# Weight tiles halved one tile after their fetch, and an output projection that starts with the attention heads, in a one-core decoder layer

## The chip, the cores and the metric

The kernel runs on one core of a Trainium2 chip. The metric is the device time of one launch in microseconds (us). Before the change it is 2632.16 us (median of three runs, 2631.33 to 2634.64).

The engines are named as the profile names them: PE multiplies matrices (PEld loads its stationary operand), DVE and POOL work elementwise, ACT scales, copies and takes sigmoids, and SP issues most of the DMAs. Each engine runs its own list of instructions strictly in the listed order; a semaphore makes an instruction wait for another engine or for a DMA.

## The reference

One trunk layer on `x` of 2048 tokens by 1024 channels, all in float32:

```python
a = rmsnorm(h, g_pre_mix)
u = a @ w_in                       # conv value | conv gate | q | k | v, 512 columns each
conv_out = silu(layernorm(causal_depthwise_conv31(val * sigmoid(gate)) + conv_b))
# stick-breaking attention, 8 heads of 64, no softmax; z = q k / 8:
log_1m = where(mask, log_sigmoid(-z), 0)
between = reverse_cumsum(log_1m) - log_1m
attn = where(mask, exp(log_sigmoid(z) + between), 0)
attn_out = headwise_rmsnorm(attn @ v, attn_norm_g)
y = concat([conv_out, attn_out]) @ w_out
h = h + rmsnorm(y, g_post_mix)
f_in = rmsnorm(h, g_pre_ffn)
f = (silu(f_in @ w_gate) * (f_in @ w_up)) @ w_down        # 2816 hidden channels
h = h + rmsnorm(f, g_post_ffn)
```

## The kernel before

**Precision.** [...] 

**Tiles and stages.** The tokens are worked in four groups `g` of 512. A table `PLAN` lists the main stages in order: `qkv` and `gv` are the input projection (`inproj`) of a group, `mix` gathers the two branches of a group, `out` is the output projection (`outproj`), and `fprep`, `c11` and `p4` are first parts of the feed-forward products. Each stage is a Python generator; a helper `beside` emits, between its steps, steps of three side generators: the attention (`attn`), the convolution (`taps`, then `convnorm`) and sums of feed-forward weights (`sums`). A step that needs a result first yields a `need`, and sides are emitted until it is there.

What is emitted earlier has priority, but the lists of the engines are made by a scheduler that simulates the engines and their buffers: the listed order can differ from the emitted one, and a small edit can move instructions hundreds of rows away. The hardware then follows the lists.

**Attention.** Work is counted in *scores*: one score is one tile of 128 queries against up to 512 keys of one head. It is two matmuls into `z` (L558, L559), two sigmoids on ACT (`om` L564, `A` L566), a scan on DVE (L568), a multiply on POOL (L569), four transposes of `A` on PE (`at`, L585), a split of those into `TH` and `TL` (L245, L246), and two matmuls into `o` (L590, L591). There are 320 scores, with four `om` buffers between them. "Dense" matmuls are those of the main stages: `inps`, `ops`, `c` (c11) and `p` (p4).

**Weights.** `Weights.next` hands out weight tiles of 128 by 1024. It calls `load_w` for up to `ahead` tiles beyond the one in use. `load_w` issues the DMA into `raw` (two buffers, L206), the copy to `wH` on ACT (L207) and, the first time a tile is used, the subtraction to `wL` on POOL (L211, one instruction of 1024 columns), whose result is also stored in DRAM (L213). At a later use of the same tile `wL` is loaded instead (L209). `half_w` does the same on 512 columns for `p4` (L222 to L224).

**The mixer.** `mix(g)` waits for `conv` and `attn` of its group, takes the two-buffered `xH`/`xL` tiles, and splits eight blocks: k = 0 to 3 from the convolution, loaded from DRAM into `m` (L519), and k = 4 to 7 from the attention, which lie on chip as `ma`. ACT makes `xH` (L523), DVE `xL` (L524). `outproj` multiplies by `w_out` in two column halves `e`; each half takes k = 0 to 3 first and k = 4 to 7 second. The first part is copied out on ACT (L688), the second is added on DVE (L690).

**The five products.** After the last output projection, `five` runs 44 blocks of Strassen-like products numbered 6, 5, 7, 4 and 3 (4 is left out where `p4` has it already). Its weights are the stored sums of pairs, (6, 5) and (7, 3); each pair is loaded into a `raw` tile (L1049), copied to `wH` (L1060) and subtracted on POOL (L1061), one block ahead. For the first blocks the remaining `residual` parts and `input_sums` are emitted between the products; `input_sums` ends in splits of `piece` (L802, L803). The tag `row` has four buffers: in `five` it holds one tile with `c11` and `p4` or a22 data per block (`ra`, loaded by L1043, L1116, L1117 and others), the `xr` and `junk` rows of a residual, and in the second half the `a22h` tile.

Of the kernel before, what the change touches and what calls it, by code (L numbers as in the profile page):

```python
# [18 lines left out]
P = 128  # L19
S = 2048  # L20
D = 1024
# [114 lines left out]
def layer_kernel(ctx: ExitStack, tc: tile.TileContext, x, xT, g_pre_mix, w_in, conv_w, conv_b, ln_g, ln_b,  # L136
# [61 lines left out]

    def load_w(w):

        src, n = w
        H = wp.tile([P, D], F32R, tag="wH", name="wH", bufs=3)
        L = wp.tile([P, D], F32R, tag="wL", name="wL", bufs=3)
        key = id(src), n
        raw = wp.tile([P, D], F32, tag="raw", name="raw")
        nc.sync.dma_start(raw, src[n])  # L206
        nc.scalar.activation(H, raw, AF.Copy)  # L207
        if key in kept:
            nc.sync.dma_start(L.bitcast(F32), kept[key])  # L209
            return H, L  # L210
        nc.gpsimd.tensor_tensor(L, raw, H.bitcast(F32), ALU.subtract)  # L211
        kept[key] = dp.tile([P, D], F32, name=f"wL_{len(kept)}")
        nc.sync.dma_start(kept[key], L.bitcast(F32))  # L213
        return H, L

    def half_w(w):

        src, n = w
        r = wp.tile([P, D], F32, tag="raw", name="raw")
        H = wp.tile([P, D], F32R, tag="wH", name="wH", bufs=3)  # L220
        L = wp.tile([P, D], F32R, tag="wL", name="wL", bufs=3)
        nc.sync.dma_start(r[:, 0:G], src[n][:, G:2 * G])  # L222
        nc.scalar.activation(H[:, 0:G], r[:, 0:G], AF.Copy)
        nc.gpsimd.tensor_tensor(L[:, 0:G], r[:, 0:G], H[:, 0:G].bitcast(F32), ALU.subtract)  # L224
        return H, L

    class Weights:


        def __init__(self, srcs, ahead=2, load=load_w):  # L230
            self.srcs = list(srcs)
            self.load = load
            self.tiles = []
            self.n = 0
            self.ahead = ahead

        def next(self):
            while len(self.tiles) < min(self.n + 1 + self.ahead, len(self.srcs)):
                self.tiles.append(self.load(self.srcs[len(self.tiles)]))
            self.n += 1  # L240
            return self.tiles[self.n - 1]

# [268 lines left out]
    def mix(g, tiles=None):  # L511

        yield need(("conv", g), ("attn", g))
        Hs, Ls = xtiles() if tiles is None else tiles()
        mc[g] = (Hs, Ls)
        for k in range(KT):
            if k < CB:
                m = ev("m")
                nc.sync.dma_start(m, conv[g][:, k, :])  # L519
            else:  # L520
                m = ma[g, k - CB]
            H = Hs[k // CB][:, k % CB, :]
            nc.scalar.activation(H, m, AF.Copy)  # L523
            nc.vector.tensor_tensor(Ls[k // CB][:, k % CB, :], m, H.bitcast(F32), ALU.subtract)  # L524
        done.add(("mix", g))
        yield 1
# [461 lines left out]
    with ExitStack() as E:  # L988
# [48 lines left out]
        def weights(g, i, j, A):  # L1037
# [9 lines left out]
            for ns in ((6, 5), (7, 3)):  # L1047
                r = wp.tile([P, D], F32, tag="raw", name="raw")
                nc.sync.dma_start(r, stored["S", i, j, ns].rearrange("p n t -> p (n t)"))  # L1049
                raws.append((r, ns))  # L1050
# [331 lines left out]
```

## Time and profile before

| what | value |
|---|---|
| median of the runs shown | 2632.16 us |
| time of the profiled execution | 2632.4 us |
| its span, first to last instruction | 2630.6 us |
| mean granted PE clock | 0.970 |
| PE busy | 2460.1 us, 94% |
| DVE busy | 1859.7 us, 71% |
| POOL busy | 1482.0 us, 56% |
| ACT busy | 1290.7 us, 49% |

The profile is one execution. Busy time counts an instruction from its start to its end; matmuls overlap, so PE can be busy without running at its peak. A row of a group reads: line, engine, operation, written tile, read tiles, shapes, count, busy time in total, mean of one in ns, and the idle time of the engine right before, with what ended it. In the chain of waits the work is followed back from the last instruction. "Granted clock" is the share of the full PE clock that the throttle passed.

By stretches, the stages lie so: mixed projections, attention and feed-forward parts from 0 to 1527 us, the last output projection to about 1586 us, `five` to about 2178 us, then the down projection.

### The profile page before, as it was taken

The page shows a single profiled execution, that of the slowest core. Times are in us where ns is not written, and L with a number is a line of the kernel's source. Part 1 is how long each engine was busy: PE and PEld are TensorE (multiplying, and loading weights), DVE is VectorE, ACT ScalarE, POOL GpSimd, SP SyncE. Part 2 cuts the span into 40 slices and gives each one's busy share as a digit, 9 for nine tenths or more (in the row PEclk, how much of TensorE's full clock was granted, in tenths as well). Part 3 has the DMA queues.
Part 4 walks back from the last instruction along what each step waited for, and adds up shares of the span by engine and source line. Part 5 has one row for each costly group of instructions (what it writes and reads, how often), then busy time and mean ns, then how long its engine had stood idle before and what let it go on. Part 6 is the DMA issues. An engine that isn't in the chain of part 4 may idle for free.

```text
span 2630.6 us, 35776 instructions
## 1 busy us (share of the span) xinstructions
PE 2460.1 (94%) x11156; PEld 1970.1 (75%) x11156; DVE 1859.7 (71%) x2409; ACT 1290.7 (49%) x2395; POOL 1482.0 (56%) x1844
## 2 busy tenths in 40 slices
PE   8889989997999999999999989889999999999998
PEld 6777867785777778777788767667777777887886
DVE  5787569977999676687765538877776665557556
ACT  4455546656564565557666643333322224444543
POOL 6654587557765656548534406675534434557556
PEclk9999989998999999989999989999999999999999
DMA  9999869986798788856777646887665557668654
GB/s 343 330 305 308 286 221 314 358 285 219 255 350 262 251 306 277 293 168 224 264 255 231 203 152 216 315 270 242 206 210 184 193 199 271 194 196 271 210 190 170
DMA packets 289182, 657.32 MB, mean 250 GB/s; under 512 B 33888, under 2 KB 42080, under 8 KB 288992
## 3 DMA queue, kind: packets, MB, share of 16 engines
q1 hardware_dynamic: 264704, 622.01, 70.8%
q10 hardware_dynamic: 24288, 33.04, 3.5%
q8 instruction: 88, 1.44, 0.2%
q14 instruction: 102, 0.84, 0.1%
HBM read 460.92 MB, written 193.99 MB: 249 GB/s over the span
## 4 chain that ended last, share of the span: by engine, by line
PE 61%; DVE 15%; DMA 10%; POOL 6%; issue 5%; ACT 2%; SPq 1%; POOLq 0%; DVEq 0%; ACTq 0%
PE b L755 16%; PE dps L755 13%; PE c L755 9%; DVE om L568 3%; PE at L585 3%; DVE cv L473 2%; PE inps L253 2%; PE inps L255 2%; PE inps L257 2%; PE p L755 2%; PE o L591 2%; PE z L558 2%; PE ops L686 1%; PE ops L684 1%; PE ops L685 1%
## 5 line engine op out<-in xcount | busy, mean ns | idle before, releaser
L569 POOL TENSOR_TENSOR A<-A,om 128x512 f32<-128x512 f32 (+2 forms) x320 | 314.4, 983 | 356.5 <-DVE om L568 314.8
L568 DVE TENSOR_TENSOR_SCAN om<-om,one,z 128x513 f32<-128x513 f32 (+2 forms) x320 | 351.5, 1112 | 115.1 <-ACT A L566 103.1
L1061 POOL TENSOR_TENSOR wL<-raw,wH 128x512 fp32r<-128x512 f32 x176 | 257.2, 1489 | 283.7 <-ACT wH L1060 283.7
L473 DVE SCALAR_TENSOR_TENSOR cv<-glu,cw,cv 128x512 f32<-128x512 f32 x464 | 346.4, 746 | 5.8
L1241 DVE TENSOR_TENSOR xL__22087<-t__22089,xH__22086 128x512 fp32r<-128x512 f32 x154 | 197.8, 1293 | 159.2 <-ACT xH__22086 L1240 159.2
L1239 POOL TENSOR_TENSOR xL__22085<-t__22088,xH__22084 128x512 fp32r<-128x512 f32 x154 | 207.6, 1353 | 176.1 <-ACT xH__22084 L1238 175.5
L253 PE MATMUL inps<-xH,wL 128*128 128x512 f32 x640 | 262.2, 410 | 4.3 <-DVE qkL L246 4.0
L255 PE MATMUL inps<-xH,wH 128*128 128x512 f32 x640 | 259.0, 405 | 0.0
L257 PE MATMUL inps<-xL,wH 128*128 128x512 f32 x640 | 258.6, 405 | 0.0
L564 ACT ACTIVATE om<-z 128x512 f32<-128x512 f32 (+2 forms) x320 | 171.0, 536 | 164.9 <-DVE z L561 67.3
L246 DVE TENSOR_TENSOR TL<-at,TH 128x512 fp32r<-128x512 f32 (+1 forms) x320 | 189.2, 598 | 85.4 <-ACT TH L245 84.7
L755 PE MATMUL dps<-xH__22084,xL__22087 128*128 128x512 f32 x616 | 241.6, 392 | 6.8 <-DVE xL__22087 L1241 5.6
L755 PE MATMUL dps<-xL__22085,xH__22086 128*128 128x512 f32 x616 | 241.3, 392 | 3.9 <-POOL xL__22085 L1239 3.9
L755 PE MATMUL dps<-xH__22084,xH__22086 128*128 128x512 f32 x616 | 241.0, 391 | 0.0
L839 POOL TENSOR_TENSOR sum<-sum 128x512 f32<-128x512 f32 x132 | 172.2, 1305 | 104.3 <-DMA sum<-in_w_down_dram 37.5
L207 ACT ACTIVATE wH<-raw 128x1024 fp32r<-128x1024 f32 x156 | 165.6, 1062 | 104.1 <-DMA raw<-in_w_in_dram 42.7
L245 ACT ACTIVATE TH<-at 128x512 fp32r<-128x512 f32 (+1 forms) x320 | 167.7, 543 | 90.8 <-PE at L585 82.5
L1238 ACT ACTIVATE xH__22084<-t__22088 128x512 fp32r<-128x512 f32 x154 | 97.1, 631 | 232.8 <-POOL xL__22085 L1239 145.0
L585 PE MATMUL at<-idr,A 128*128 128x128 f32 x1088 | 194.2, 283 | 10.9 <-ACT ma L625 3.6
L585 PEld LDWEIGHTS at<-idr,A 128*128 128x128 f32 x1088 | 143.7, 146 | 48.8 <-POOL A L569 5.9
L566 ACT ACTIVATE A<-z 128x512 f32<-128x512 f32 (+2 forms) x320 | 167.5, 537 | 21.3 <-PE at L585 19.6
L558 PE MATMUL z<-K,QL 128*128 128x512 f32 (+2 forms) x320 | 132.4, 415 | 29.4 <-DVE om L568 24.0
(303 smaller groups left out, 6283.3 us busy)
## 6 DMA issues: line engine op xcount, KB each, us to landing
wL<-wL SPq DMA_DIRECT2D x156, 512.0 KB, 4.7
raw<-in_w_in_dram SPq DMA_DIRECT2D x80, 512.0 KB, 5.9
t__22089<-u SPq DMA_DIRECT2D x154, 256.0 KB, 2.8
c<-c ACTq DMA_DIRECT2D x88, 256.0 KB, 3.9
t__22088<-wd SPq DMA_DIRECT2D x88, 256.0 KB, 2.9
K<-kd SPq DMA_DIRECT2D x80, 256.0 KB, 4.5
V<-vd SPq DMA_DIRECT2D x80, 256.0 KB, 4.1
u<-accf SPq DMA_DIRECT2D x22, 768.0 KB, 4.1
```

Of the source, the lines that this page charges most:

```text
L246: nc.vector.tensor_tensor(L, ps, H.bitcast(F32), ALU.subtract)
L253: nc.tensor.matmul(ps, WL[:, kc], aH[t](k), start=k == 0, stop=False)
L255: nc.tensor.matmul(ps, WH[:, kc], aH[t](k), start=False, stop=False)
L257: nc.tensor.matmul(ps, WH[:, kc], aL[t](k), start=False, stop=k == KT - 1)
L473: nc.vector.scalar_tensor_tensor(to, gl[c][:, k:k + G], cw[:, c, k:k + 1], a, ALU.mult, ALU.add))
L568: nc.vector.tensor_tensor_scan(r, r, z[:, 0:1].to_broadcast([P, w + 1]), one, ALU.mult, ALU.bypass)
L569: nc.gpsimd.tensor_tensor(a[:, 0:w], a[:, 0:w], om[:, G - w + 1:G + 1], ALU.mult)
L585: nc.tensor.transpose(pt[:, j * P:(j + 1) * P], u["A"][j][:, b * P:(b + 1) * P], id32)
L755: return nc.tensor.matmul(ps, a, b, skip_group_check=True, **flags)
L1061: nc.gpsimd.tensor_tensor(l, t, f32(h), sub)
L1239: nc.gpsimd.tensor_tensor(WL, w, f32(WH), sub)
L1241: nc.vector.tensor_tensor(UL, t, f32(UH), sub)
```

## The change

1. `load_w` only allocates and fetches. The halving is put into a closure `halves`, which `Weights.next` calls one tile later: up to `ahead - 1` tiles beyond the one in use instead of `ahead`. For `c11` (`ahead` = 1) it is called for the tile in use.
2. The subtraction on POOL is done in pieces of 512 columns instead of one of 1024.
3. `half_w` becomes `load_w` with an offset.
4. `mix` issues the four loads of `m` first, then splits the attention blocks k = 4 to 7, then the convolution blocks k = 0 to 3.
5. `outproj` takes k = 4 to 7 first in both column halves, and fetches its weight tiles in that order.
6. In `five` the (7, 3) pair is loaded into a `row` tile, and only the (6, 5) pair into `raw`.

```diff
-    def load_w(w):
+    def load_w(w, lo=0):
         src, n = w
+        raw = wp.tile([P, D], F32, tag="raw", name="raw")
         H = wp.tile([P, D], F32R, tag="wH", name="wH", bufs=3)
         L = wp.tile([P, D], F32R, tag="wL", name="wL", bufs=3)
-        key = id(src), n
-        raw = wp.tile([P, D], F32, tag="raw", name="raw")
-        nc.sync.dma_start(raw, src[n])
-        nc.scalar.activation(H, raw, AF.Copy)
-        if key in kept:
+        m = D - lo
+        nc.sync.dma_start(raw[:, 0:m], src[n][:, lo:D])
+        key = id(src), n, lo
+        known = key in kept
+        if known:
             nc.sync.dma_start(L.bitcast(F32), kept[key])
-            return H, L
-        nc.gpsimd.tensor_tensor(L, raw, H.bitcast(F32), ALU.subtract)
-        kept[key] = dp.tile([P, D], F32, name=f"wL_{len(kept)}")
-        nc.sync.dma_start(kept[key], L.bitcast(F32))
-        return H, L
+        def halves():
+            nc.scalar.activation(H[:, 0:m], raw[:, 0:m], AF.Copy)
+            if known:
+                return
+            for i in range(0, m, G):
+                ks = slice(i, i + G)
+                nc.gpsimd.tensor_tensor(L[:, ks], raw[:, ks], H[:, ks].bitcast(F32), ALU.subtract)
+            if not lo:
+                kept[key] = dp.tile([P, D], F32, name=f"wL_{len(kept)}")
+                nc.sync.dma_start(kept[key], L.bitcast(F32))
+        return H, L, halves
...
         def next(self):
             while len(self.tiles) < min(self.n + 1 + self.ahead, len(self.srcs)):
                 self.tiles.append(self.load(self.srcs[len(self.tiles)]))
             self.n += 1
-            return self.tiles[self.n - 1]
+            while self.made < min(self.n + self.ahead - 1, len(self.srcs)):
+                self.tiles[self.made][2]()
+                self.made += 1
+            return self.tiles[self.n - 1][:2]
...
-        for k in range(KT):
-            if k < CB:
-                m = ev("m")
-                nc.sync.dma_start(m, conv[g][:, k, :])
-            else:
-                m = ma[g, k - CB]
+        ms = [ev("m") for _ in range(CB)] + [ma[g, p] for p in range(CB)]
+        for k in range(CB):
+            nc.sync.dma_start(ms[k], conv[g][:, k, :])
+        for k in (*range(CB, KT), *range(CB)):
...
-        wts = Weights([(w_out, n) for n in range(KT)])
+        order = range(CB - n, -1, -n)
+        wts = Weights([(w_out, CB * e + kp + i) for e in range(2) for kp in order for i in range(n)])
         for e in range(2):
             es = slice(e * G, (e + 1) * G)
-            for kp in range(0, CB, n):
+            for kp in order:
...
-                    if kp == 0:
+                    if kp == order[0]:
...
             for ns in ((6, 5), (7, 3)):
-                r = wp.tile([P, D], F32, tag="raw", name="raw")
+                r = wp.tile([P, D], F32, tag="raw", name="raw") if ns[0] == 6 else row("raw2")
```

The lists of the engines move in many places. Three of them matter below.

ACT at the second mixer (`mix(1)`), the copies from `m` and `ma` to `xH`. Before, they stand together, with a few instructions of the attention among them:

```order
L564 ACTIVATE om<-z 128x384
L523 ACTIVATE xH<-m 128x512
L523 ACTIVATE xH<-ma 128x512 x4
L564 ACTIVATE om<-z 128x512
L523 ACTIVATE xH<-m 128x512
L245 ACTIVATE TH<-at 128x512
```

Now three of the `ma` copies stand some 90 rows ahead of that, and the fourth 16 rows behind these three:

```order
L568 ACTIVATE om<-z 128x384
L251 ACTIVATE TH<-at 128x512 x2
L568 ACTIVATE om<-z 128x512
L527 ACTIVATE xH<-ma 128x512 x3
L214 ACTIVATE wH<-raw 128x1024
```

The `m` copies are at the old place:

```order
L568 ACTIVATE om<-z 128x512
L251 ACTIVATE TH<-at 128x512 x2
L527 ACTIVATE xH<-m 128x512 x3
L251 ACTIVATE TH<-at 128x512
L527 ACTIVATE xH<-m 128x512
L570 ACTIVATE A<-z 128x384
```

So four of the eight copies left the place at which the output projection begins, and the other four stayed.

PE at the end of the last `c11`, the last dense matmuls ahead of the end of the attention. Before, 4 scores of 320 are listed behind the last of these rows:

```order
L755 MATMUL c_17039<-xL,wH 128x512
L590 MATMUL o<-TH,V 128x512
L591 MATMUL o<-TL,V 128x512
L585 MATMUL at<-idr,A 128x128 x4
L590 MATMUL o<-TH,V 128x512
```

Now 12 scores are listed behind it, and the last transposes of the convolution too (`cps`):

```order
L760 MATMUL c_17089<-xL,wH 128x512
L509 MATMUL cps<-idr,cs 128x128 x4
L594 MATMUL o<-TH,V 128x512
L595 MATMUL o<-TL,V 128x512
L589 MATMUL at<-idr,A 128x128 x2
```

So the dense work runs ahead of the attention by eight scores more at this point. Counted through the two lists of PE, the stretches of more than six scores with neither a dense matmul nor `tps` transposes in them, together with the one at the end, are, before, 19 scores (105 to 124), 8 (220 to 228) and 4 (316 to 320); now 16 (108 to 124), 14 (217 to 231) and 12 (308 to 320).

ACT in `five`, around the last split of a `piece`. Before:

```order
L802 ACTIVATE e__18249<-piece 128x512
L1060 ACTIVATE wH<-raw 128x512 x4
L802 ACTIVATE e__18249<-piece 128x512
L1060 ACTIVATE wH<-raw 128x512 x2
L802 ACTIVATE t__19439<-sumin 128x512
```

Now:

```order
L807 ACTIVATE e__18299<-piece 128x512
L1065 ACTIVATE wH<-raw_18600 128x512 x2
L1065 ACTIVATE wH<-raw 128x512 x2
L807 ACTIVATE e__18299<-piece 128x512
L807 ACTIVATE t__19489<-sumin 128x512
```

Counted from the start of `five`, 22 pairs of `wH` copies stood ahead of the last split of a `piece`, and 23 do now; each of the four splits has one pair more ahead of it.

More of the change, by code (lines that the diff above doesn't have):

```diff
@@ L197, in layer_kernel @@
     kept = {}
[L199 removed]
+    def load_w(w, lo=0):
         src, n = w
+        raw = wp.tile([P, D], F32, tag="raw", name="raw")
         H = wp.tile([P, D], F32R, tag="wH", name="wH", bufs=3)
         L = wp.tile([P, D], F32R, tag="wL", name="wL", bufs=3)
[L204 to L225 removed]
+        m = D - lo
[3 more added lines that the diff above has]
+        if known:
+            nc.sync.dma_start(L.bitcast(F32), kept[key])
+        def halves():
[9 more added lines that the diff above has]
+        return H, L, halves
+    def half_w(w):
+        return load_w(w, G)
     class Weights:
@@ L234, in __init__ @@
             self.n = 0
+            self.made = 0
             self.ahead = ahead
@@ L1047, in weights @@
             for ns in ((6, 5), (7, 3)):
-                r = wp.tile([P, D], F32, tag="raw", name="raw")
+                r = wp.tile([P, D], F32, tag="raw", name="raw") if ns[0] == 6 else row("raw2")
                 nc.sync.dma_start(r, stored["S", i, j, ns].rearrange("p n t -> p (n t)"))
```

4 lines of the change are left out of this document (2 added, 2 removed).

## The prediction

> **What bounds the kernel now.** I read the page first, then the table by stretches, then the waits and the order in time of the stretches in which PE is not full.
>
> ```profile
> span 2630.6 us, 35776 instructions
> PE 2460.1 (94%) x11156; PEld 1970.1 (75%) x11156; DVE 1859.7 (71%) x2409; ACT 1290.7 (49%) x2395; POOL 1482.0 (56%) x1844
> ```
>
> PE is busy for 94% of the span, and the change neither adds nor removes a matmul. So it can only act on PE's idle time, 2630.6 - 2460.1 = 170 us, and on the clock that PE is granted. The execution took 2632.4 us, 1.8 more than its span and 0.2 more than the median of the runs, 2632.16; I count from 2632.4.
>
> The table by stretches tells where PE falls behind (columns: stretch, length, then busy time and count of PE, PEld, DVE, ACT and POOL, granted clock, DMA share, GB/s):
>
> ```profile
> 342.30:370.30 28.00, 20.75 (x79) 16.75 (x77) 23.11 (x29) 13.97 (x29) 19.08 (x23) 0.76 0.72 230
> 605.50:645.90 40.40, 31.62 (x143) 21.97 (x142) 33.00 (x50) 25.95 (x56) 32.69 (x59) 0.87 0.66 203
> 645.90:666.40 20.50, 14.49 (x58) 10.20 (x57) 18.51 (x27) 12.67 (x26) 11.84 (x20) 0.92 0.61 199
> 1124.10:1143.70 19.60, 16.12 (x59) 10.88 (x58) 17.68 (x28) 11.73 (x23) 9.80 (x16) 0.74 0.71 216
> 1320.00:1386.00 66.00, 66.00 (x324) 54.12 (x323) 45.91 (x62) 40.01 (x73) 20.25 (x49) 1.00 0.75 249
> 1492.70:1503.50 10.80, 8.44 (x36) 6.04 (x35) 6.98 (x7) 7.68 (x15) 4.08 (x9) 0.84 0.70 233
> 1700.00:1730.00 30.00, 21.91 (x88) 16.95 (x86) 26.18 (x33) 10.08 (x19) 17.57 (x13) 0.90 0.91 311
> ```
>
> Where attention and dense work are mixed, as from 1320 to 1386, PE is full at clock 1.00. It falls behind in three kinds of places: at the three mixers inside the attention (from 342, 646 and 1124), in stretches of attention alone (605 to 646, 1493 to 1504), and in the first blocks of `five` (1700 to 1730).
>
> A stretch of attention alone shows in the groups of PE within it: no dense line is among its larger groups, and 16 scores pass (L559 x16).
>
> ```profile
> L585 PE MATMUL at<-idr,A 128*128 128x128 f32 x58 | 11.1, 296 | 1.3 <-POOL A L569 1.3
> L558 PE MATMUL z<-K,QL 128*128 128x512 f32 (+3 forms) x17 | 8.8, 518 | 5.3 <-DVE om L568 5.3
> L559 PE MATMUL z<-K,QH 128*128 128x512 f32 (+3 forms) x16 | 6.7, 421 | 0.0
> ```
>
> PE waits most for the scan (L568) that gives an `om` buffer back: here the chain through ACT, DVE and POOL sets the pace.
>
> **The change, part by part.** *The mixers.* These rows show the first one (ACT and PE, in order of time) and the second:
>
> ```profile
> 344.72 0.63 ACT L523 ACTIVATE xH<-m 128x512 fp32r<-128x512 f32 x1 [5.70 <-DMA m<-conv]
> 345.25 0.96 ACT L245 ACTIVATE TH<-at 128x512 fp32r<-128x512 f32 x2
> 345.89 0.79 PE L590 MATMUL o<-TH,V 128*128 128x512 f32 x1 [2.74 <-ACT TH L245]
> 350.27 2.18 ACT L523 ACTIVATE xH<-ma 128x512 fp32r<-128x512 f32 x4
> 649.16 0.63 ACT L523 ACTIVATE xH<-m 128x512 fp32r<-128x512 f32 x1 [2.60 <-DMA m<-conv]
> 650.57 0.50 PE L684 MATMUL ops<-wH,xL 128*128 128x512 f32 x1 [2.27 <-DVE xL L524]
> ```
>
> ACT runs in order, so its 5.70 us wait for the convolution's load also held the attention's `TH`, and PE with it. The loss of a mixer is its idle time plus the share of its busy time that the clock took: (28.00 - 20.75) + 20.75 x 0.24 = 12.2 us at the first, (20.50 - 14.49) + 14.49 x 0.08 = 7.2 at the second, (19.60 - 16.12) + 16.12 x 0.26 = 7.7 at the third, 27 together. At the first mixer four head copies (2.18 us) and a `TH` (0.96) now stand ahead of the first copy from `m`: 3.1 of the 5.70 us, 55%, so 6.7 of 12.2. At the second the four head copies have left the place, while the load and its wait stay: I take half, 3.6. At the third the four loads are listed one by one among other DMAs, as before: a third, 2.6. Sum 13 us saved. Bounds: 0, if the load gates the in-order queue all the same, and 27.
>
> [...]
>
> *The fourth mixer*, after the attention, splits three head blocks, four `m` and the last head block, eight copies as before:
>
> ```profile
> 1525.89 2.18 ACT L523 ACTIVATE e__17216<-m 128x512 fp32r<-128x512 f32 x4
> ```
>
> The first product can start behind the first copy in both kernels; the last head block is copied eighth, 8 x 0.545 = 4.4 us on, when PE has nine slow matmuls behind it. Zero, at most 1 us lost.
>
> *The order of dense work and attention.* The scheduler's list has moved. By the counts beside the lists above, the stretches of scores without dense work grow from 19 + 8 + 4 = 31 to 16 + 14 + 12 = 42. In the mixed part a score costs PE its own work. Row prices: a 512-wide matmul 285.29 / 1212 = 0.235 us, a transpose 0.60 / 4 = 0.15 us:
>
> ```profile
> 1879.29 285.29 PE b L755 x1212
> 606.62 0.60 PE L585 MATMUL at<-idr,A 128*128 128x128 f32 x4
> ```
>
> A score is four matmuls and four transposes, 0.94 + 0.60 = 1.54 us. Alone it takes 40.40 / 16 = 2.53 us. So each bare score wastes 0.99 us, and 11 more of them cost 11 us, most at the end of the attention (8 more) and behind the first half of the third output projection (6 more). Bounds: 0, if the other engines catch up elsewhere; 16, by the dearer pace of 10.80 / 4 = 2.70 us and three scores more in the stretches with `tps`. That half an output projection can run before the convolution is done gives nothing further: it is already in these counts.
>
> *The halves one tile later.* In the lists the copies hardly move: a `wH` copy stands on average 4.8 scores ahead of its first matmul before, 5.0 now, and as far behind its load as before. PE's cover is three tiles of weights. Zero. If they were late, ACT's wait for `raw` would be late next:
>
> ```profile
> ACT wH L207 <- DMA raw<-in_w_in_dram: 42.7, 14, 6.0
> L211 POOL TENSOR_TENSOR wL<-raw,wH 128x1024 fp32r<-128x1024 f32 x50 | 120.3, 2407 | 54.6 <-ACT wH L207 53.5 <-DMA kd<-qkH 1.0
> L224 POOL TENSOR_TENSOR wL<-raw,wH 128x512 fp32r<-128x512 f32 x22 | 28.4, 1296 | 5.6 <-ACT wH L223 5.3 <-ACT om L564 0.2
> ```
>
> *The narrower pieces* make one POOL instruction of 2407 ns into two of 1296: 185 ns more, 50 times, 9 us of POOL. POOL is idle 44% of the span; what hides it is that idle time, and without cover it would be 9. In the bare stretch POOL is busy 32.69 of 40.40, so I take 1.
>
> *The (7, 3) pair in `row`.* In `five` PE and SP wait for the halving of weights:
>
> ```profile
> PE b L755 <- POOL wL L1061: 14.0, 7, 6.0
> SPq L1049 <- POOL wL L1061: 72.2, 31, 8.9
> 1726.73 0.63 ACT L802 ACTIVATE e__18249<-piece 128x512 fp32r<-128x512 f32 x1 [12.13 <-DVE piece L918]
> 1727.27 1.13 ACT L1060 ACTIVATE wH<-raw 128x512 fp32r<-128x512 f32 x2
> 1730.89 0.79 PE L755 MATMUL b<-xH__17525,wL 128*128 128x512 f32 x1 [6.00 <-POOL wL L1061]
> ```
>
> The longest PE wait, 6.00 us, is a pair whose copies stood on ACT behind a split that waited 12.13 us for DVE. With one pair more ahead of each such split that wait should go. But DVE is busy 26.18 of 30.00 us there and is late next: I take 5 of the 14.0 us. Bounds: 14 saved; and 9 lost, since `row` now holds one tile more per block and SP already waits for its buffers:
>
> ```profile
> SPq L1043 <- DVE sumf L1068: 9.4, 4, 3.6
> ```
>
> **Sum:** -13 - 5 + 11 + 1 = -6, so 2632.4 - 6 = 2626 us. All terms at their good ends give -41, all at their bad ends +35.
>
> **The rivals.** *Slower: the end of the attention decides.* Twelve bare scores at the end instead of four, and six more behind the third mixer, while the loads of `m` gate ACT as before: 11 + 1 us lost, nothing saved, 2644. For it: the `m` loads stand at the same place of SP's list at mixers two and three, and a lost score cannot be hidden once the dense work is gone. Against it: the 5.70 us wait of the first mixer has work ahead of it now. It decides as soon as mixers and `five` together give less than 12 us.
>
> *It cancels: 2632.* The mixers give 7 and `five` 4, and the bare scores take that back. For it: gains and losses come from the same shift, dense work ahead of attention; also the halving does not do what its words say, since the lists place it where it was.
>
> *Much faster: 2602.* The mixers give 22 of their 27 us because the clock stays up, `five` gives 9, and the bare scores cost nothing because DVE, with fewer splits at the mixers, passes the scores faster: 2632.4 - 31. Against it: DVE is busy 33.00 of 40.40 us in the bare stretch, where no mixer takes its time.
>
> **How the numbers follow.** Forecast 2626 (own range 2619 to 2629): 0.36. Much faster: 0.10. Cancelling: 0.28. Slower: 0.26. About 0.2%, 5 us, is what a measurement of this kernel can tell from no change, so faster is 0.36 + 0.10 = 0.46, same 0.28, slower 0.26. The range reaches from the edge of the much faster case to just past the slower one: 2606 to 2645.
>
> **What would show each step.** At the first mixer the wait of ACT's copy from `m` should be under 3 us and PE's wait for `TH` gone; at the second the wait of 2.27 us for `xL` may stay, with the clock up behind it. Before the last output projection PE should show 12 scores without a `c` matmul, some 30 us instead of 11. In `five`, PE's wait for `wL` should be under 9 us and the one of 6.00 us absent; waits for DVE should have grown. POOL's pieces should take near 1296 ns. The prediction is wrong if the scores of the bare stretches take less than 2.2 us, if SP blocks on `row` buffers so that PE waits for the (7, 3) pair, or if the granted clock of the span falls below 0.970.

## The result and the profile after

The changed kernel takes 2647.64 us (median of four runs, 2645.83 to 2655.61), the kernel before, run beside it, 2631.74 (2630.92 to 2634.64). The ratio is 1.0063 with a 95% interval of 1.005 to 1.0075: by the ratio 16.6 us slower, where I had forecast 6 us faster. The time also lies outside my range, 2606 to 2645.

The head of the page of the changed kernel:

```profile
span 2645.3 us, 35841 instructions
PE 2462.8 (93%) x11156; PEld 1969.2 (74%) x11156; DVE 1840.2 (70%) x2409; ACT 1293.5 (49%) x2395; POOL 1487.6 (56%) x1894
```

The work is the same; PE's idle time has grown from 170 to 182 us, and the granted clock is 0.972. The table by stretches of the changed kernel (columns: stretch, length, busy time and count of PE, PEld, DVE, ACT and POOL, granted clock, DMA share, GB/s):

```profile
315.00:345.00 30.00, 29.29 (x144) 23.57 (x143) 21.80 (x28) 21.66 (x41) 26.35 (x35) 1.00 0.81 279
576.00:597.00 21.00, 7.52 (x24) 5.88 (x24) 7.66 (x9) 4.64 (x9) 16.04 (x23) 0.64 0.59 197
610.00:652.40 42.40, 32.83 (x143) 22.93 (x142) 32.18 (x49) 26.62 (x57) 34.01 (x59) 0.85 0.72 224
652.40:678.40 26.00, 20.70 (x90) 15.91 (x89) 21.36 (x31) 12.92 (x24) 13.61 (x22) 0.91 0.65 203
1144.00:1155.90 11.90, 8.96 (x28) 6.12 (x27) 11.24 (x16) 9.11 (x18) 7.40 (x13) 0.71 0.78 271
1490.00:1514.30 24.30, 19.75 (x92) 12.82 (x91) 18.75 (x22) 18.25 (x36) 14.32 (x33) 1.00 0.55 185
1700.00:1730.00 30.00, 26.04 (x111) 20.88 (x110) 26.18 (x30) 10.00 (x18) 21.99 (x15) 0.89 1.00 359
```

The first mixer (from 315) hardly holds PE: 29.29 of 30 us busy at clock 1.00. (The output projection behind it waits once more, for a weight; see below.) But a hole of 21 us stands at 576, where PE is busy 7.52 us. The waits at the second and third mixers (652, 1144) are much as they were.

Two traces whose lists differ cannot be laid beside each other by the clock on the wall. I compared them at equal work of PE: each row of PE is given the price that it has where PE is full (the lower quartile of the time to the next row, by form, in the trace of before), and the prices are summed. Every kernel here comes to 2261 to 2263 us of work that way. Elapsed time minus work is *lost time*, and it can be told by stretches that hold the same amount of work in each kernel. The borders in the next table are 475, 540, 935, 1240 and 1290 us of work; in the kernel before they lie at 581, 688, 1154, 1484 and 1564 us. Each row of the table is worked out from one profiled execution. Two executions of one and the same edit (b_heads and its repeat) differ by at most 2.4 us in a column. That is a single pair, and the profiled execution need not be a typical one: in b_heads (2623.04 us, median 2629.38), heads_slot (2619.49, 2628.07) and b_wide (2650.32, 2662.03) it was the fastest of its runs. So the columns tell where time goes, and the ratios of the runs tell how much.

| kernel | to 475 | 475 to 540, second mixer | 540 to 935, third mixer | 935 to 1240 | 1240 to 1290, end of attention | rest | all |
|---|---|---|---|---|---|---|---|
| before, lost time | 98.8 | 41.5 | 71.8 | 24.3 | 30.5 | 84.6 | 351.4 |
| the change, against before | -23.2 | +14.3 | +10.8 | +2.3 | +8.1 | +1.5 | +13.8 |

So the change has a large gain first, 23.2 us up to the second mixer, and then gives back 14.3 there, 10.8 on the way to the third mixer and 8.1 at the end of the attention. The stretch of the second mixer, in the kernel before and in the changed one (their waits and clock differ, the work of PE is the same):

```profile
581.30:687.80 106.50, 85.94 (x396) 64.17 (x395) 85.94 (x122) 61.95 (x121) 79.09 (x123) 0.92 0.73 234
558.00:678.80 120.80, 90.37 (x393) 67.51 (x392) 85.97 (x122) 64.54 (x124) 82.36 (x127) 0.86 0.68 216
```

The hole at 576 us, seen on PE in order of time, the rows with a wait ahead of them (the last part of a row is the idle time and what ended it):

```profile
583.98 0.80 PE L689 MATMUL ops<-wH,xL 128*128 128x512 f32 x1 [8.04 <-DVE glu L430]
593.69 1.09 PE L627 MATMUL po<-idr,ot 128*128 128x128 f32 x4 [5.49 <-DVE ot L619]
```

And on POOL at the same time:

```profile
572.37 1.27 POOL L844 TENSOR_TENSOR sum<-sum 128x512 f32<-128x512 f32 x1
579.56 1.26 POOL L844 TENSOR_TENSOR sum<-sum 128x512 f32<-128x512 f32 x1 [5.92 <-DMA sum<-in_w_gate_dram]
580.78 0.86 POOL L573 TENSOR_TENSOR A<-A,om 128x384 f32<-128x384 f32 x1
...
582.99 0.21 POOL L429 COPY glu<-glu 128x30 f32<-128x30 f32 x1
```

This is a chain of queues. POOL has a sum of feed-forward weights (L844, work of the side generator `sums`, needed only in the last products, which start at 1594 us) at the head of its list, and waits 5.92 us for the load. Behind it stand the attention's products (L573) and a small copy of the convolution (L429). DVE's `glu` (L430) waits 8.09 us for that copy, and the output projection needs a PSUM bank of the kind that `glu` reads from (in the code both take theirs from the tag `mm`). So PE waits 8.04 us, and the dense work that could fill the time has run out. The row of 5.49 us is the same once more: the head norm's `ot` waits for `ss` from POOL (DVE's own wait is 0.85 us, the row on POOL runs from 590.13 us for 1.64), which stands behind further sums of 1.29 and 1.26 us.

An earlier wait comes from the same queue. In the first output projection PE waits 5.73 us for the low half of a `w_out` tile (the high half `wH` is ACT's copy of the tile, the low half `wL` is the tile minus `wH`, and a product is three matmuls, here `wH` by `xL`, `wH` by `xH` and `wL` by `xH`); no such row is in the kernel before. The rows on PE and POOL:

```profile
366.59 0.79 PE L691 MATMUL ops<-wL,xH 128*128 128x512 f32 x1 [5.73 <-POOL wL L219]
```

```profile
352.36 10.01 POOL L368 TENSOR_TENSOR xcol<-xcol,rb 128x512 f32<-128x512 f32 x8
...
365.27 4.96 POOL L219 TENSOR_TENSOR wL<-raw,wH 128x512 fp32r<-128x512 f32 x4
```

In POOL's order the halving of this tile, the sixth of `w_out`, stands behind 10 us of scaling for a later input projection (`xcol`). In the kernel before it stands behind the same block (subtraction at 394.16 us, `xcol` from 380.69 to 391.72), but there PE comes to the tile later and does not wait. So a part of PE's early lead is lost again at once.

### The profile page after: what moved, and what is told of

It reads as the page before. It is cut to its first block, busy times and chain, and to the rows that moved or that the text cites. A ratio compares the mean times of both kernels' runs of the same rounds, so it can differ in the third digit from the quotient of the medians.

```text
span 2645.3 us, 35841 instructions
## 1 busy us (share of the span) xinstructions
PE 2462.8 (93%) x11156; PEld 1969.2 (74%) x11156; DVE 1840.2 (70%) x2409; ACT 1293.5 (49%) x2395; POOL 1487.6 (56%) x1894
## 5 line engine op out<-in xcount | busy, mean ns | idle before, releaser
L573 POOL TENSOR_TENSOR A<-A,om 128x512 f32<-128x512 f32 (+2 forms) x320 | 312.5, 977 | 340.8 <-DVE om L572 310.3
L1066 POOL TENSOR_TENSOR wL<-raw,wH 128x512 fp32r<-128x512 f32 x176 | 255.4, 1477 | 303.5 <-issue 158.7
L844 POOL TENSOR_TENSOR sum<-sum 128x512 f32<-128x512 f32 x132 | 171.7, 1301 | 121.4 <-DMA sum<-in_w_down_dram 36.1
L214 ACT ACTIVATE wH<-raw 128x1024 fp32r<-128x1024 f32 (+1 forms) x178 | 179.4, 1008 | 117.7 <-DMA raw<-in_w_in_dram 41.4
L1065 ACT ACTIVATE wH<-raw 128x512 fp32r<-128x512 f32 x176 | 101.0, 623 | 208.1 <-PE b L760 123.1
L219 POOL TENSOR_TENSOR wL<-raw,wH 128x512 fp32r<-128x512 f32 x122 | 159.0, 1322 | 48.9 <-ACT wH L214 44.2
```

The costliest lines, as they stand in the source:

```text
L573: nc.gpsimd.tensor_tensor(a[:, 0:w], a[:, 0:w], om[:, G - w + 1:G + 1], ALU.mult)
L1066: nc.gpsimd.tensor_tensor(l, t, f32(h), sub)
```

## The experiments

Three theories stood at the start, and a fourth, D, came with the first traces. **A**: what counts is the number of scores that pass without dense work, some 1 us lost for each. **B**: the later halving and its pieces cost time themselves. **C**: the `row` slot costs it. **D**: the sums on POOL, where the list has put them, hold POOL's queue ahead of the second mixer. Every edit is on the kernel before unless said otherwise; ratios are to the kernel before on the same chip, with 95% intervals.

### The parts alone

*b_heads*: edits 4 and 5 (the whole of `mix` and `outproj` as in the change).

> The kernel before with edits 4 and 5 alone (loads of m first, head blocks first in the mixer and in the output projection). Theory A, the order of the list decides: the list of PE now has 40 scores without dense work (18 at 108 to 126, 13 at 218 to 231, 9 at 311 to 320) where the kernel before has 31; 9 more at 0.99 us are 9 us lost, and of the first mixer's stall some 10 us are saved only to be given back at the second group, as in the changed kernel; 2637 to 2645. Theory B, the later halving and its narrower pieces cost the time: this kernel keeps only the mixers' gain, 2617 to 2628. Theory C, the row slot in the last products costs it: also 2617 to 2632.

Measured: 2629.38 us, ratio 0.9983 (0.9968 to 0.9998). The profiled execution lost 9.1 us less than before. By A this kernel should have been slower; the cost of the change is not in these edits. (The time is just above B's range and within C's.) A repeat of the same edit (the label names a pin that it does not have):

> The kernel with edits 4 and 5 once more, one look on this chip beside the others: 2623 to 2632.

Measured, one run: 2625.31 us.

*b_late*: edits 1 to 3.

> The kernel before with edits 1 to 3 alone (halves one tile later, in pieces of 512, half_w as a case of load_w). The list of PE has 25 scores without dense work at 104 to 129, 16 at 212 to 228 and 4 at the end, 45 where the kernel before has 31. Theory A, the order of the list decides: 14 more at 0.99 us, 2640 to 2650. Theory B, the late halving itself costs: 2640 to 2650 as well, but with PE waiting for wH or wL in the dense stretches, over 10 us more of it than before. Theory C, the row slot costs it: 2632.

Measured: 2654.13 us, ratio 1.0076 (1.0056 to 1.0097), 4 us above the end of A's and B's ranges. This is the part that makes the change slow. But PE hardly waits for weights in it. All waits of PE for weights before 1560 us in b_late:

```profile
PE p L761 <- POOL wL L219: 1.7, 1, 1.7
PE inps L259 <- DMA wL<-wL: 1.0, 1, 1.0
PE ops L692 <- DMA wL<-wL: 1.0, 1, 1.0
```

Together 3.7 us, against 5.3 in the kernel before. B in its plain form, that PE waits for late halves, does not explain the 20 us of b_late. In the changed kernel the same sum is 10.8 us, of which the wait of 5.73 us above is the largest part; in heads_slot, which is the changed kernel without edits 1 to 3, it is 7.7.

*b_out* and *b_mix*: edit 5 alone and edit 4 alone.

> The kernel before with edit 5 alone (the output projection takes the head blocks first, the mixer is as before). The list of PE has 16, 16 and 9 scores without dense work, 41 where the kernel before has 31, and the first matmul of each output projection now needs the blocks that the mixer splits last. Theory A: 10 us lost and nothing saved at the mixers, 2638 to 2646. Theories B and C: no change, 2630 to 2634.

Measured: 2636.09 us, ratio 1.0011 (0.9998 to 1.0023), between the theories: of A's 10 us some 3 are there.

> The kernel before with edit 4 alone (the mixer loads m first and splits the head blocks first; the output projection keeps its order). The end of the attention keeps its 4 scores without dense work; 17 and 12 at the second and third mixer, 33 in all against 31. Stage by stage from the kernels run so far: the mixers' gain up to PE work 475 as with edits 4 and 5 together (-8), -7 before the second mixer, the end of the attention 0 instead of +5: 2616 to 2624, the fastest so far. If the gain of edits 4 and 5 together needs the head blocks' products first: 2630 to 2636.

Measured: 2638.88 us, ratio 1.0017 (1.0005 to 1.0029). Each alone gains nothing in the whole, both together do. Why is not shown: counted the same way, edit 4 alone already gains some 7 us up to the second mixer, as both together do, and loses some 12 between the second and the third. My expectation, put together from the columns of other kernels, missed by 15 us from the end of its range; columns of different kernels do not add up.

*b_slot*: edit 6.

> The kernel before with edit 6 alone (the (7, 3) pair in a row tile). The lists are the same up to the last products. My prediction had 5 us saved there: 2627. Theory C, the slot costs time: 2634 to 2641, with PE waiting in the first blocks for products of DVE or for wL. Theories A and B leave it within 2 us of 2632.

Measured: 2631.97 us, ratio 0.9992 (0.9976 to 1.0008). C is out. The waits of PE in its first blocks of `five` (1578 to 1800 us):

```profile
PE b L755 <- DVE cs L1068: 7.3, 4, 3.9
PE b L755 <- DVE cy L1068: 4.3, 4, 1.8
PE b L755 <- POOL wL L1061: 4.1, 3, 2.5
PE b L755 <- DVE glu L1068: 3.7, 3, 1.4
```

The waits for `wL` fall as forecast, from 13.1 us in the same stretch of the kernel before to 4.1. DVE is late next, as forecast too: its three rows here grow from 9.7 to 15.3 us and take 5.6 of the 9.0 back.

*b_narrow* and *b_wide*: edits 1 to 3 taken apart.

```diff
-        nc.gpsimd.tensor_tensor(L, raw, H.bitcast(F32), ALU.subtract)
+        for i in range(0, D, G):
+            ks = slice(i, i + G)
+            nc.gpsimd.tensor_tensor(L[:, ks], raw[:, ks], H[:, ks].bitcast(F32), ALU.subtract)
```

> The kernel before with edit 2 alone, two subtractions of 512 columns in place of one of 1024. Its list has 37 scores without dense work (21, 12 and 4). My prediction had 1 us for the pieces themselves. Theory A: six more scores, 2636 to 2640. If the pieces are what costs in edits 1 to 3 together: 2648 to 2656. If nothing of this counts: 2632.

Measured: 2650.34 us, ratio 1.0077 (1.0052 to 1.0103), in the range for pieces that cost by themselves.

> The kernel before with edits 1 and 3 alone, the subtraction still one instruction of 1024 columns. Its list has 38 scores without dense work (18, 16 and 4). Theory A: 7 more than before at 0.99 us, 2637 to 2642. Theory B, the later halving itself costs: near the 2654 of edits 1 to 3 together. If the pieces are what costs there: 2630 to 2634.

Measured: 2662.03 us, ratio 1.0111 (1.0088 to 1.0134), above all three ranges. Each half of edits 1 to 3 costs as much as both together. That is no sum of two costs; it speaks for the list. b_narrow shows the hole of the changed kernel once more, by the waits of PE and POOL between 571 and 660 us:

```profile
PE cps L505 <- POOL cs L500: 7.8, 1, 7.8
```

```profile
POOL sum L841 <- DMA sum<-in_w_up_dram: 10.3, 2, 7.1
```

### The sums held back

*after_pin* is the changed kernel with the sums from the eighth hidden tile on tied to the second mixer: a copy of one column that depends on the mixer's result goes ahead of their first load.

```diff
-SUMS = ((330, 0.0), (900, 1.0))
+SUMS = ((330, 0.0), (391, 0.42), (440, 0.43), (900, 1.0))
...
+                if (j, i) == (7, 0):
+                    yield need(("mix", 1))
+                    late_.append(mc[1][0][0][:, 0, 0:1].bitcast(F32))
                 a21, a22, a11 = piece(w, j + HF, 0), piece(w, j + HF, 1), piece(w, j, 0)
...
             t = fup.tile([P, G], F32, tag="sum", name="sum", bufs=3)
+            while late_:
+                nc.gpsimd.tensor_copy(t[:, 0:1], late_.pop())
```

> The changed kernel, with POOL's sums of feed-forward weights from the eighth hidden tile on held back until the second mixer (a small copy that depends on the mixer's xH goes ahead of their first load). POOL's list then has 7 sums in the 48 scores 80 to 128, where it had 40. Theory D, sums that wait for their loads hold POOL's queue while the dense work has run out: the two waits of 8.0 and 5.5 us before the second mixer go, 12 to 18 us less than the changed kernel, 2628 to 2636. Theory A, the number of scores without dense work: 41 by this list against 42 of the changed kernel, so 2645 to 2649.

Measured: 2633.82 us, ratio 1.0003 (0.9988 to 1.0018). The changed kernel has 1.0063, so holding the sums back is worth 0.6%, 16 us. The stretch from 475 to 540 us of work, shown above for the changed kernel, is with the sums held back:

```profile
555.60:656.30 100.70, 86.42 (x384) 66.79 (x383) 78.86 (x111) 61.31 (x116) 57.31 (x98) 0.86 0.46 144
```

This is the same work of PE in 100.7 us instead of 120.8, with POOL 25 us less busy. PE's longest waits there are now

```profile
PE z L562 <- DVE om L572: 4.2, 8, 1.3
PE o L594 <- ACT TH L251: 3.1, 2, 2.5
PE cps L509 <- POOL cs L504: 3.1, 1, 3.1
```

The waits of 8.04 and 5.49 us are gone. That settles the hole at 576 us: it is D. (The wait of 5.73 us for `wL` in the first output projection stays, with 5.77 us.) It does not settle the whole, as the same edit on three other kernels shows.

> The kernel before with the same edit on the sums. Its list has 37 scores without dense work (19, 14 and 4) against 31. Theory D: it loses only the 4.3 us that PE waited for DVE and POOL at that place, 2622 to 2630. Theory A: six more scores at 0.99 us, 2636 to 2640.

Measured: 2643.67 us, ratio 1.0048 (1.003 to 1.0065). Here D fails by some 14 us, and A is nearer.

> Edits 1 to 3 alone, with POOL's sums held back until the second mixer. Edits 1 to 3 lost 14.6 us in the stretch before the second mixer and 15.5 before the third. Theory D: the first of these goes, with some 5 more as in the other kernels with the sums held back, and part of it comes back before the third mixer, where PE now arrives earlier: 2630 to 2644. If the later halving itself holds PE: 2652 to 2656.

Measured: 2645.79 us, ratio 1.0048 (1.0032 to 1.0064), 2 us above D's range; b_late had 1.0076.

> The kernel before with edit 2 alone and POOL's sums held back until the second mixer. Theory D: the 13.7 us that edit 2 lost before the second mixer go (0 to -5 against the kernel before), 2632 to 2642 in all, since its list has 16 scores at the third mixer and 8 at the end without dense work. If the pieces cost by themselves: 13 us lost in that stretch still, 2648 to 2656.

Measured: 2661.0 us, ratio 1.0102 (1.0083 to 1.0122), 19 us above D's range; b_narrow had 1.0077.

| lost time against before | to 475 | 475 to 540 | 540 to 935 | all |
|---|---|---|---|---|
| the change | -23.2 | +14.3 | +10.8 | +13.8 |
| after_pin | -25.8 | -5.8 | +26.1 | -2.8 |
| b_late | -9.6 | +14.6 | +14.6 | +23.0 |
| late_pin | -11.8 | -2.0 | +24.0 | +11.5 |
| b_narrow | -9.8 | +13.7 | +12.3 | +14.8 |
| b_narrow_pin | -3.6 | +3.4 | +33.9 | +32.5 |
| before_pin | -4.8 | -9.2 | +22.5 | +11.4 |

In each pair the second mixer gets 9 to 20 us cheaper, and the next stretch 9 to 23 us dearer. So holding the sums back makes the second mixer cheaper in all four, but only the changed kernel is clearly faster by it as a whole. The sums have to be made somewhere; what PE wins at the second mixer it mostly loses again on the way to the third.

*after_tp* tests that last point by itself: the changed kernel, in which the third mixer is made free earlier.

```diff
-    ("c11", 0, 121, ("hscaled", 1, 1, 0), ("tprep", 0, 4, 4)),
+    ("c11", 0, 121, ("hscaled", 1, 1, 0), ("tprep", 0, 1, 2)),
```

> The changed kernel with the sums of the feed-forward inputs of group 0 emitted earlier within c11(0), so that the third mixer is free earlier. Its list has 16 scores without dense work at 108 to 124, none at the third mixer, and 28 at the end of the attention (292 to 320) where the changed kernel has 16, 14 and 12. If scores without dense work set the time wherever they stand: the loss before the third mixer falls by some 15 us, the loss at the end of the attention grows by as much or more, 2644 to 2656. If the third mixer is a loss of its own: 2630 to 2636.

Measured: 2645.53 us, ratio 1.0049 (1.0032 to 1.0065). In the stretch of the third mixer it loses 24.2 us less than the changed kernel, and after it 26.2 us more (22.9 from 935 to 1240 and 3.3 at the end of the attention). PE now has these waits between 1100 and 1180 us, and no others:

```profile
PE ops L689 <- ACT big L693: 0.7, 1, 0.7
PE o L595 <- DVE TL L252: 0.2, 1, 0.2
```

Here a hole that is closed in one place opens in another: moving the scores without dense work gained nothing clear of the intervals.

### Edits 1 and 2 undone in the changed kernel

*after_wide* has one subtraction of 1024 columns again, *after_early* calls `halves` as soon as a tile is fetched.

```diff
-            for i in range(0, m, G):
-                ks = slice(i, i + G)
+            for i in range(0, m, D):
+                ks = slice(i, min(i + D, m))
...
-            while self.made < min(self.n + self.ahead - 1, len(self.srcs)):
+            while self.made < min(self.n + self.ahead, len(self.srcs)):
```

> The changed kernel without edit 2 (one subtraction of 1024 columns). POOL's list has 12 sums in the scores 80 to 96, as many as with the losses of 14 us (10 to 14 of them), while the kernels without that loss have 7. Theory D: 14 us lost before the second mixer although the pieces are gone, 2640 to 2652. If the pieces are the cause: that loss gone, 2630 to 2636.

Measured: 2657.94 us, ratio 1.0101 (1.0078 to 1.0123).

> The changed kernel without the delay of edit 1 (halves called as soon as the tile is fetched). POOL's list has 11 sums in the scores 80 to 96. Theory D: 14 us lost before the second mixer, 2640 to 2652. If the delay is the cause: 2625 to 2636.

Measured: 2645.92 us, ratio 1.0052 (1.0031 to 1.0072).

*heads_slot* is the changed kernel without edits 1 to 3 (edit 3 was not taken out by itself).

> The changed kernel without edits 1 to 3 (the kernel before with edits 4, 5 and 6). Sum of the ratios measured apart: -4.5 for edits 4 and 5 and -2 for edit 6, so 2625, range 2619 to 2631, faster than both kernels. If the three need each other: 2632 to 2647.

Measured: 2628.07 us, ratio 0.9984 (0.9969 to 0.9999): the same as b_heads, faster than the changed kernel by 0.8%, and than the kernel before by 0.16%, which is less than the 0.2% taken as no change.

| lost time against before | to 475 | 475 to 540 | 540 to 935 | end of attention | all |
|---|---|---|---|---|---|
| after_wide | +3.8 | +3.6 | +16.0 | +7.8 | +27.8 |
| after_early | -10.0 | -1.3 | +21.1 | +7.6 | +19.4 |
| b_wide | +1.6 | -2.5 | +19.3 | 0.0 | +17.3 |
| heads_slot | -10.4 | -5.8 | +0.1 | +6.9 | -11.4 |

Undoing edit 1 or edit 2 leaves the kernel as slow as it was or slower; undoing both, with edit 3, removes the loss. Beside heads_slot, the changed kernel gains 12.8 us up to the second mixer and loses 20.1 at it and 10.7 on the way to the third: there lies what edits 1 to 3 cost. I had expected 14 us to be lost at the second mixer in after_wide and after_early, since their lists hold about as many sums there as the list of the change. They lose 3.6 and -1.3, so the number of sums at that place does not tell where a hole opens. The time of after_early lies in D's range all the same and that of after_wide 6 us above it, for another reason: 21 and 16 us lost on the way to the third mixer.

### A shift of the list with no other edit

What edits 1 and 2 have in common is that they move the list. These two runs move it with no edit to the weights at all: the line that says how far the attention is emitted ends 5 units later or earlier.

```diff
-ATTN = ((100, 0.0), (905, 1.0))
+ATTN = ((100, 0.0), (910, 1.0))
```

> The kernel before with the attention's line ending at 910 instead of 905: same instructions, another list, with 16 and 18 scores without dense work at the second and third mixer (19 and 8 before) and none but the last at the end. If edits 1 and 2 cost by shifting the list and the list of before is a favourable one: as slow as they are, 2640 to 2660, the loss between the second and third mixer up by 10 to 20 us. If their cost is their own: 2628 to 2636.

Measured: 2636.38 us, ratio 1.0024 (1.0009 to 1.004), between the two ranges. (Counted again, its list has 6 scores without dense work at the end, 40 in all.)

> The same with 900: 23 and 18 scores without dense work at the second and third mixer. If any shift of the list costs: 2640 to 2665. If edits 1 and 2 cost by themselves: 2628 to 2638.

Measured: 2662.28 us, ratio 1.0123 (1.0099 to 1.0147).

| lost time against before | to 475 | 475 to 540 | 540 to 935 | all |
|---|---|---|---|---|
| attn910 | -0.3 | -1.7 | +12.3 | +11.3 |
| attn900 | +0.5 | +9.0 | +13.6 | +28.6 |

The same instructions with the same operands, in another order, cost 0.24% and 1.23%, mostly in the same stretches as edits 1 and 2. In attn900 POOL waits there (555 to 700 us) for the sums' loads as in the changed kernel:

```profile
POOL sum L839 <- DMA sum<-in_w_gate_dram: 16.1, 3, 6.8
```

So the 0.5 to 1.1% that edits 1 and 2 cost in their various forms is within what a mere shift of the list can cost here. It does not prove that they cost nothing by themselves; two shifts are few, and one of them cost less than any form of edits 1 and 2. The list of the kernel before seems a favourable one: of all the kernels here only those with edits 4 and 5 together and without 1 to 3 were faster than it by more than their interval.

## Why the prediction was wrong

**The step that failed** is the pair "the halves one tile later: zero" and "the narrower pieces: I take 1". Alone, these edits cost 20 us (0.0076 of 2632, 15 to 26 by the interval). The parts measured apart give -4.5 (edits 4 and 5), +20.0 (1 to 3) and -2.1 (6), together +13.4; the change gives +16.6. So the parts nearly add up in total, and the sum missed mainly by this one term; taking edits 1 to 3 out of the changed kernel (heads_slot) gives the same amount back, 0.8%. What I had reasoned about it was partly wrong and not enough. "Zero" for the later halves rested on PE's cover of three tiles; in the changed kernel that cover fell short once, for 5.73 us in the first output projection, where PE waits for POOL's `wL` in the output projections 0.9 us in heads_slot, 0.4 in after_wide and not at all in after_early. For the rest PE hardly waits for weights, and the pieces cost POOL no more than I had put down (they now take

```profile
L219 POOL TENSOR_TENSOR wL<-raw,wH 128x512 fp32r<-128x512 f32 x122 | 159.0, 1322 | 48.9 <-ACT wH L214 44.2
```

1322 ns in the mean, where I had 1296; POOL is busy 5.6 us more in all). I priced what the two edits *do* and left out that they make the scheduler write another list. For the shift of the list I had one term, the count of scores without dense work, with bounds of 0 and 16. It left out what the list does to the other queues: where POOL meets a sum whose load is late, and which chain stands behind it. That is shown for the hole at 576 us, which goes when the sums are held back. That the rest of the 20 us comes from the list too is argued from attn910 and attn900 and not shown.

**The order of dense work and attention, +11.** The place was right and the price too high. At the end of the attention the change has 12 scores without `c` as forecast, but they pass (to the last `z`, as the 10.80 us of before were taken) within the 24.30 us of the row above, at clock 1.00, not in 30. That is 2.0 us a score, below the 2.2 that I had named as a sign of being wrong; the 16 scores from 610 us took 42.40 / 16 = 2.65. The loss there is 8.1 us; every kernel with the new order of the output projection has 4.7 to 11.4 there (edits 4 and 5: 5.4, and 4.7 in the repeat; edit 5 alone: 5.7), and those with the old order have -1.4 to 3.8. As a measure for the whole kernel the count fails: attn910 and b_heads both have 40 such scores, nine more than before, and by the medians of the runs the one is 0.24% slower than before and the other 0.17% faster.

**The mixers, -13.** At the first mixer the wait that I named went as told: ACT's waits for `m` between 310 and 345 us are

```profile
ACT xH L527 <- DMA m<-conv: 2.8, 2, 1.9
```

and PE's wait for `TH` is gone. The gain up to the second mixer is 8.0 us in b_heads (5.6 in the repeat) where I had 6.7. That this is so near is in part luck. Of the 7.25 us that PE was idle there in the kernel before, ACT's wait for `m` explains 2.74. The other 4.51 were a wait for `TL`, which DVE made behind three splits of head blocks:

```profile
361.17 0.58 PE L591 MATMUL o<-TL,V 128*128 128x256 f32 x1 [4.51 <-DVE TL L246]
```

```profile
355.80 4.78 DVE L524 TENSOR_TENSOR xL<-ma,xH 128x512 fp32r<-128x512 f32 x3
```

My 55% was a share of ACT's wait, applied to both; in b_heads both waits are gone. Of the 23.2 us that the change gains up to the second mixer, the mixers explain only these 6 to 8. b_late gains 9.6 there with edits 1 to 3 alone, for which I had no term and have no cause. At the second mixer the wait for `xL` stayed, as I had said it might:

```profile
PE ops L689 <- DVE xL L528: 3.8, 1, 3.8
```

At the third nothing was gained. In b_heads and its repeat the mixers give 5.6 to 8.0 and 5.5 to 6.7 at the first two, and the end of the attention takes back about 5. Forecast for edits 4 and 5 with the list's term: -13 + 11 = -2; measured -4.5, with an interval from -8.4 to -0.5.

**The (7, 3) pair in `row`, -5.** The mechanism was right. The size is not settled: alone the edit saves 2.1 us, with an interval from 6.3 saved to 2.1 lost, which still holds my 5. In the changed kernel the waits of PE in the last products (from 1514 us) are

```profile
PE b L760 <- DVE cs L1073: 8.9, 5, 4.0
PE b L760 <- DVE glu L1073: 7.9, 5, 2.8
PE b L760 <- DVE cy L1073: 6.5, 5, 1.8
PE b L760 <- POOL wL L1066: 6.3, 3, 2.5
```

The one of 6.00 us is absent and `wL` stands at 6.3 us instead of 14.0. The three rows of DVE come to 23.3 us; before they were 17.4 together:

```profile
PE b L755 <- DVE glu L1068: 6.9, 5, 2.3
PE b L755 <- DVE cs L1068: 6.0, 3, 3.0
PE b L755 <- DVE cy L1068: 4.5, 4, 1.6
```

Of 7.7 us saved 5.9 come back as waits for DVE. I had named DVE as late next and still kept 5 of the 14.

**The rivals.** "Slower, 2644" came nearest in time. Its mechanism is not what happened: it had nothing saved at the mixers and the end of the attention decide, while the change saves 23.2 us up to the second mixer and loses 25.1 from there through the third, so its nearness is luck. "It cancels" had gains and losses come from the same shift of dense work ahead of the attention. At the hole of 576 us that fits: PE has come early and no dense work is left. But the losses lie at the second and third mixer and not, as I had it, in the count of bare scores.

**What stays open.** Holding the sums back gives 16 us of the changed kernel back. Why the new lists lose 11 to 21 us more between the second and the third mixer I have not shown. It happens in kernels with edits 1 or 2 and in attn910 and attn900 alike. In these last two it goes with the list alone, since nothing else differs; that it is the same in the others is likely and not proved, and which rows of the list do it is open.

## What to carry to other kernels

Where a scheduler writes the lists, an edit has two prices: what it does, and what it does to the list. The second can be sampled before anything else by edits that do nothing but shift the list; here two of them cost 0.24% and 1.23%, 6 and 32 us, where the largest term of my sum was 13. A gain below that cannot be told from luck with the order. A lead of PE is no gain until it has passed the next place at which the dense work must wait (here 23.2 us were gained up to the second mixer, and 25.1 lost from there through the third), so compare two traces at equal work of PE and follow the lead to the end. And background work with loads of its own can hold a latency chain that stands behind it in the same queue: here one late load of 5.92 us on POOL became a wait of 8.04 us on PE.

## What the runs showed of the hardware that I had not expected

The granted clock was low behind two long waits of PE (0.50 and 0.51), and also in two places with short waits only (0.68 and 0.50). Four stretches around the hole of the changed kernel:

```profile
575.50:584.00 8.50, 0.46 (x3) 0.02 (x2) 0.76 (x2) 1.19 (x2) 4.44 (x9) 0.67 0.79 264
584.00:588.00 4.00, 4.00 (x9) 2.80 (x9) 3.43 (x5) 0.63 (x1) 3.85 (x8) 0.50 0.56 176
588.00:594.00 6.00, 0.51 (x3) 0.34 (x3) 2.49 (x2) 0.63 (x1) 5.84 (x7) 0.78 0.34 124
594.00:599.00 5.00, 4.76 (x19) 4.08 (x18) 2.98 (x4) 3.92 (x8) 3.48 (x4) 0.51 0.72 215
```

After the waits of 8.04 and 5.49 us the next work of PE ran at half clock, 0.50 and 0.51, though PE was full or nearly so (4.00 of 4.00 and 4.76 of 5.00 us). The nine matmuls of `ops` behind the wait of 8.04 us start 0.43 us apart (the first two 0.60), those from 599.08 us on 0.23. So that place cost some 1.8 us beside the wait itself (an estimate, 9 x 0.20). That the wait brought the clock down is not shown. In the kernel before, two stretches show a low clock without such a wait:

```profile
342.30:350.00 7.70, 4.96 (x18) 3.86 (x16) 4.62 (x6) 4.75 (x10) 4.17 (x5) 0.68 0.81 269
...
625.00:630.00 5.00, 4.38 (x12) 3.12 (x13) 4.37 (x5) 3.00 (x7) 4.83 (x10) 0.50 0.53 166
```

The first holds the wait of 2.74 us and no longer wait; in the second, and in the 20 us ahead of it, no wait of PE is longer than 1.02 us. At the end of the attention of the changed kernel, in contrast, PE was busy only 19.75 of 24.30 us, with a longest wait of 1.4 us, and kept clock 1.00. So in these rows the length of PE's waits alone does not tell the clock. In the prediction the clock of 0.76 belongs to the whole first mixer, 342 to 370 us; the wait of 4.51 us for `TL` stands later in that stretch than the one of 2.74 us, so the row of 342 to 350 us, with 0.68, is the one to set beside the wait of 2.74 us.
